# Attention pairs with more in flight, merge weights turned on the matmul engine, gates by Silu, and three smaller moves in a hybrid attention and HGRN2 block

## The chip, the cores and the metric

One core of a Trainium2 chip runs the whole program in one launch. The metric is the device time of one execution in microseconds (us). The kernel before has a median of 1483.52 us over three runs (1483.29 to 1485.46).

## The reference, cut to what matters

One encoder layer on x (1024 tokens, 1024 channels), all in float32:

```python
h = rms_norm(x, norm_w);  z = h @ w_in                     # 1024 -> 12288 columns
qkv_a, g_a, q_b, zf_fwd, zf_bwd, i_b, g_b, zgate_a, zgate_b = split(z)
for g, (window, dilation) in enumerate(((128, 1), (512, 4), (2048, 16))):
    q, k = rms_norm(q_g), rms_norm(k_g)                    # 8 heads of 64 per group
    s = q @ k + bias, banded;  m = max(s);  p = exp(s - m);  den = sum(p);  o_g = p @ v / den
M = max over g of m_g;  w_g = den_g * exp(m_g - M)
o_a = sum(w_g * o_g) / sum(w_g)                            # the three groups merged per head
y_a = (o_a * silu(g_a)) @ w_proj_a
f = lb + (1 - lb) * sigmoid(zf)                            # 8 heads of 128, forward and backward
o_b = rms_norm(gated_scan_fwd + gated_scan_bwd) * silu(g_b)
y_b = o_b @ w_proj_b
out = x + (sigmoid(zgate_a) * y_a + sigmoid(zgate_b) * y_b) @ w_out
```

## The kernel before

**Products.** A float32 product is made of three matmuls on rounded halves: each operand is split into a high part (ScalarE copies it into the rounded type) and a low part (the difference), and the kernel adds high x high, high x low and low x high. One matmul is 128x128 weights against 512 columns. The low part of a weight page (128x512, 256 KB) is made in one of three ways: a subtraction on GpSimd, a subtraction on VectorE, or, for `low = "dma"`, ScalarE writes minus the high part and a GpSimd-issued DMA adds the page to it from HBM.

**Stages.** In order: norm of x and the value columns of the three groups (to about 150 us); the block stage (to 631 us), where the input projection is done in blocks of four weight pages with seven block products instead of eight (named 11, T1, T2, 21, T3, 22, T4, twelve matmuls each; `run_quads`); a stage of ordinary groups `gp`, 24 matmuls into one PSUM bank each, for the columns i_b and the queries q_b, into which the attention is interleaved (to about 850 us) and then the merge of the three groups (to about 940 us); the HGRN2 stage, head after head between the `gp` groups of the forget gates (to about 1270 us); the two branch projections and the output projection, the last two again with seven block products (`seven`; names sA and sE).

**Block stage.** A block is normal `q`/`k` columns (`qk`, 12 of them, followed by the head norm on ScalarE and VectorE), branch gates (`sg`), HGRN2's g_b (`gb`) or the attention's g_a (`ga`). The results go to HBM; silu(g_a) and silu(g_b) are made later: `ga_sig` and `ga_mul` in the merge, `gate` in the HGRN2 stage, each a Sigmoid on ScalarE and a product on VectorE.

**Attention.** The work goes in 24 pairs of 128-query slabs with four heads. For a pair, TensorE computes scores (`sc`), VectorE adds the bias and takes the maximum in one operation (`as`), ScalarE takes eight exponentials (`exps`, with the row sum read out after each), TensorE turns the result (`transpose_p`, `pT`), ScalarE and VectorE copy it (`apt`), and TensorE multiplies it by the values (`pv`, `o`); ScalarE copies that out (`aos`). `left["in"]` counts pairs between scores and values, `left["out"]` those behind, and the conditions on them in `scores` and `transpose_p` set how many pairs overlap.

**Merge.** Maximum and sum of the groups 1 and 2 go to HBM and back in the order of tokens (`stats_out`, `stats_in`), `alphas` makes one weight per token, head and group, `alphas_out` turns three tiles on TensorE, and the result goes to HBM and back once more (`alD`, `alL`) to come to 16 partitions. A unit of the merge (eight: four head pairs by two halves of the tokens) spreads the weights with three 16-row matmuls (`al`) and multiplies, adds and gates on VectorE and GpSimd (`spread_al`).

**What sets the order.** All instructions are written out by a planner (`Builder`) that keeps a modelled time for each engine (`Plan.note` has the cost of each operation) and issues a task when its inputs are due and its `room` condition holds. Small TensorE pieces ("products" such as `sc`, `pT`, `o`, `al`, `U`) are put between the large matmuls, after every three to six of them, when the plan says that they are ready. The engines then run their lists in order; where reality is later than the plan, an engine waits.

Every instruction is recorded by one helper, so all have its line (57), and the profile's groups are told apart by tile names: `gp`, `qA`, `qE`, `qC`, `sA`, `sE` are PSUM tiles of large products, `whi`/`wlo` weight halves, `xh`/`xl` and `hh`/`hl` those of the data, `ob` and `acc` the data of the branch projection.

Of the kernel before, what the change touches and what calls it, by code (L numbers as in the profile page):

```python
# [18 lines left out]
S = 1024  # L19
# [9 lines left out]
EARLY = 8  # L29
QRAW, SPARE = 6, 7  # L30
LOWS = ("T2", "T4")
SQ, EA = 2, 6
VR, PT = 16, 7
# [81 lines left out]
class Plan:  # L115
# [25 lines left out]
    def note(self, key, op, args, kw):  # L141
# [30 lines left out]
        else:  # L172
# [12 lines left out]
            elif key == "act":  # L185
                pace = 0.09 + n / 1200.0
                need = {AF.Sigmoid: ("sig",), AF.Ln: ("ln",), AF.Exp: ("exp", "ln")}.get(args[2])
# [396 lines left out]
def hybrid_block(ctx, tc, a, out):  # L584
# [47 lines left out]
    for k in range(6):  # L632
        blocks += qk[2 * k:2 * k + 2] + sg[k:k + 1] + ([("gb", k)] if k < 4 else [])
    blocks += [("ga", 0), ("ga", 2)]

    def block_pages(kind, *at):
        if kind == "sg":
            return (*gate_pages(*at), *gate_pages(at[0], at[1] + 1))
        if kind == "ga":
            return tuple(some(72 + 2 * at[0], 4))  # L640
        if kind == "gb":
# [11 lines left out]
    for h in range(EARLY):  # L653
        items += q_pages(h)
# [151 lines left out]
    alD = dr.tile([3, 2, 8, 8, 128], F32, name="alD")  # L806
# [309 lines left out]
    def put_raw(dst):  # L1116
        def f(half, col, z, mine):
            ring = stage
            if not mine:
                ring, ps, z = blk["spare"], z, blk["spare"].get()  # L1120
                a_.activation(z, ps, AF.Copy)
# [4 lines left out]
            b.task("sp", [z], out, 1)  # L1126
# [3 lines left out]
    put_ga = lambda j: put_raw(lambda col, half: gaD[j + col, half])  # L1130
    put_gb = lambda k: put_raw(lambda col, half: gbD[2 * k + col, half])
# [6 lines left out]
    b.run_quads(A, [{"qk": put_qk, "sg": put_sg, "ga": put_ga, "gb": put_gb}[x[0]](*x[1:]) for x in blocks],  # L1138
# [7 lines left out]
    def attention_start(now=False):  # L1146
# [17 lines left out]
        for g in range(3):  # L1164
            for hv in range(2):
                soon = lambda n, k=2 * g + hv: att[n].soon() and (k == 0 or b.wire())
# [52 lines left out]
    def score_tasks(g, hv):  # L1219
# [61 lines left out]
    def exps(g, hv, i0, u, ss, neg, geo):  # L1281
        n, c0 = geo[u][1:3]
        for h in range(4):
            a_.activation(ss[u][:, h, c0:c0 + n], ss[u][:, h, c0:c0 + n], AF.Exp, bias=neg[:, u, h:h + 1],
                          accum_out=mst[g][:, 1, i0 + u, 4 * hv + h:4 * hv + h + 1])
        if u == 0:
            left[g, hv, i0] = []
        m = left["m", g, hv, i0]
        b.product(1, [ss[u]], lambda: transpose_p(g, hv, i0, u, ss[u], [x[3] for x in geo]),
                  lambda: left["out"] == m and att["pt"].soon(2 if g < 2 else 1), banks=2 if g < 2 else 1)  # L1290

    def transpose_p(g, hv, i0, u, s, slabs):
# [30 lines left out]
        if u == 0:  # L1323
# [6 lines left out]
                  and (b.bank.room(5 if g < 2 else 3) and b.bank.when(5 if g < 2 else 3) <= b.p.t["pe"] or not b.small))  # L1330
# [30 lines left out]
    vleft = {}  # L1361
# [9 lines left out]
    def merge_maybe(now=False):  # L1371
# [8 lines left out]
        mer["sel"] = sel = mer["p"].tile([16, 4, 128], F32R, name="sel")  # L1380
        half = lambda k: ident[0:16, 8 * k:8 * k + 8].rearrange("p (a j) -> p a j", a=4)[:, :, :, None].to_broadcast([16, 4, 2, 64])
        v_.tensor_tensor(sel.rearrange("p a (j c) -> p a j c", j=2), half(0), half(1), op=OP.add)
        mer["og"] = b.ring(mer["p"], "og", 6, [128, 512])
        mer["gal"] = b.ring(mer["p"], "gal", 2, [128, 512])
        mer["gas"] = b.ring(mer["p"], "gas", 2, [128, 512])
        merge_start()

    def stats_out():
        for g in (1, 2):
            for k in range(2):  # L1390
                if g == 1:
                    for half in range(2):
                        a_.dma_start(
                            _dram(stD, ((g * 2 + k) * S + 512 * half) * 8, [[32, 128], [8, 4], [1, 8]]),
                            mst[g][:, k].rearrange("p (r e) h -> p e r h", e=2)[:, half])
                else:
                    a_.dma_start(_dram(stD, (g * 2 + k) * S * 8, [[64, 128], [8, 8], [1, 8]]), mst[g][:, k])

    def stats_in():
        for g in (1, 2):  # L1400
            for k in range(2):
                a_.dma_start(nst[g][:, k], stD[g, k].rearrange("(t p) h -> p t h", p=128))
        nst["in"] = True

    nst = {0: mst[0]}

    def alphas():
        M = mer["p"].tile([128, 8, 8], F32, name="mM")
        v_.tensor_tensor(M, nst[0][:, 0], nst[1][:, 0], op=OP.max)
        v_.tensor_tensor(M, M, nst[2][:, 0], op=OP.max)  # L1410
        den = mer["p"].tile([128, 8, 8], F32, name="mden")
        tmp = mer["p"].tile([128, 8, 8], F32, name="mtmp")
        es = []
        for g in range(3):
            e = mer["p"].tile([128, 8, 8], F32, name=f"me{g}")
            v_.tensor_tensor(e, nst[g][:, 0], M, op=OP.subtract)
            a_.activation(e, e, AF.Exp)
            es.append(e)
            v_.tensor_tensor(tmp if g else den, e, nst[g][:, 1], op=OP.mult)
            if g:  # L1420
                v_.tensor_tensor(den, den, tmp, op=OP.add)
        v_.reciprocal(den, den)
        for g in range(3):
            v_.tensor_tensor(es[g], es[g], den, op=OP.mult)
            x = mer["p"].tile([128, 2, 8, 8], F32R, name=f"mx{g}")
            a_.activation(x[:, 0], es[g], AF.Copy)
            v_.tensor_tensor(x[:, 1], es[g], x[:, 0].bitcast(F32), op=OP.subtract)
            es[g] = x
# [964 lines left out]
```

## Time and profile before

| | |
|---|---|
| median of three runs | 1483.52 us |
| the profiled execution, its own time | 1483.24 us |
| its span in the profile | 1481.5 us |
| granted TensorE clock | 0.999 |
| TensorE (PE) busy | 1463.4 us, 99% of the span |
| VectorE (DVE), ScalarE (ACT), GpSimd (POOL) busy | 976.3, 897.6, 369.2 us |
| DMA | 227.76 MB, 154 GB/s on average |

Between the span and the execution's own time lie 1.7 us at the start and the end. The end of a matmul is modelled in these records, so that two matmuls overlap in them: what one costs is seen from start to next start, not from its listed length.

### The profile page before, as it was taken

How to read it: one execution, taken by the hardware profiler on the slowest of the kernel's cores; microseconds unless marked ns; L12 is line 12 of the kernel's file. 1: busy time of each engine (PE TensorE's matmuls, PEld its weight loads, DVE VectorE, ACT ScalarE, POOL GpSimd, SP SyncE). 2: the span in 40 equal slices, each digit the busy share in tenths (PEclk: the TensorE clock that was granted, in tenths of full speed). 3: DMA queues.
4: the chain of work that ended last, by engine and by line, in shares of the span. 5: the costliest groups of instructions: out<-in, count | busy, mean ns of one | idle time of the engine just before them, and what ended most of it. 6: DMA issues, size and time to landing. Idle time of an engine off the chain costs nothing. (4 is left out here: it accounts for less than half of the span.)

```text
span 1481.5 us, 23010 instructions
## 1 busy us (share of the span) xinstructions
PE 1463.4 (99%) x7965; PEld 1201.1 (81%) x7965; DVE 976.3 (66%) x1890; ACT 897.6 (61%) x1889; POOL 369.2 (25%) x374
## 2 busy tenths in 40 slices
PE   8999999999999999999999999999999999999998
PEld 7788888888888888877887787788888888787887
DVE  6792676768676788434443427488988886359973
ACT  5543665657474767346766632398887885556461
POOL 0031335455433334400200324322222221000011
PEclk9999999999999999999999999999999999999999
DMA  6465567686624342475644467743445443775565
GB/s 205 133 193 166 171 199 164 160 187 130 157 79 141 79 121 79 140 260 178 202 147 143 137 159 229 225 105 92 124 98 143 108 130 91 226 230 156 162 166 134
DMA packets 193579, 227.76 MB, mean 154 GB/s; under 512 B 45564, under 2 KB 118292, under 8 KB 192949
## 3 DMA queue, kind: packets, MB, share of 16 engines
q1 hardware_dynamic: 174084, 204.06, 43.6%
q0 software_dynamic: 11952, 21.76, 9.9%
q10 hardware_dynamic: 7424, 0.45, 0.3%
q8 instruction: 63, 1.03, 0.3%
q14 instruction: 56, 0.45, 0.1%
HBM read 166.08 MB, written 81.63 MB: 167 GB/s over the span
## 5 line engine op out<-in xcount | busy, mean ns | idle before, releaser
L57 POOL TENSOR_TENSOR wlo<-qraw,whi 128x512 fp32r<-128x512 f32 x120 | 174.8, 1466 | 299.9 <-ACT whi L57 255.9
L57 ACT ACTIVATE whi<-qraw 128x512 fp32r<-128x512 f32 x168 | 104.4, 627 | 92.3 <-DVE qraw L57 40.3
L57 PE MATMUL gp<-hh,whi 128*128 128x512 f32 x336 | 139.0, 414 | 0.7 <-ACT stage L57 0.7
L57 PE MATMUL gp<-hh,wlo 128*128 128x512 f32 x336 | 131.7, 392 | 0.0
L57 PE MATMUL gp<-hl,whi 128*128 128x512 f32 x336 | 131.3, 391 | 0.0
L57 POOL TENSOR_TENSOR wlo<-raw,whi 128x512 fp32r<-128x512 f32 x48 | 66.4, 1389 | 235.8 <-ACT whi L57 233.9
L57 DVE CUSTOM_DVE_ANT_0 as<-sc,abias 128x192 f32<-128x192 f32 (+2 forms) x192 | 56.1, 348 | 100.5 <-PE sc L57 80.2
L57 DVE TENSOR_TENSOR qraw<-qraw,qraw 128x512 f32<-128x512 f32 x96 | 86.4, 901 | 35.4 <-POOL wlo L57 27.0
L57 PE MATMUL gp<-whi,hh 128*128 128x512 f32 x248 | 101.6, 410 | 2.1 <-ACT hh L57 1.4
L57 PE MATMUL gp<-whi,hl 128*128 128x512 f32 x248 | 97.6, 394 | 1.3 <-DVE hl L57 1.3
L57 PE MATMUL gp<-wlo,hh 128*128 128x512 f32 x248 | 97.5, 393 | 0.0
L57 ACT ACTIVATE whi<-raw 128x512 fp32r<-128x512 f32 x104 | 64.9, 625 | 50.8 <-PE gp L57 33.5
L57 ACT ACTIVATE as<-as,neg 128x192 f32<-128x192 f32 (+2 forms) x192 | 83.5, 440 | 6.6 <-DVE neg L57 6.6
L57 ACT ACTIVATE stage<-gp 128x512 f32<-128x512 f32 x60 | 35.5, 594 | 82.0 <-PE gp L57 57.8
L57 DVE SCALAR_TENSOR_TENSOR ny<-ny,spare 128x512 f32<-128x512 f32 x48 | 76.0, 1584 | 1.6
L57 PEld LDWEIGHTS gp<-hh,whi 128*128 128x128 f32 x336 | 63.2, 188 | 14.9 <-ACT stage L57 1.8
L57 PE MATMUL qA<-hh,whi 128*128 128x512 f32 x192 | 75.1, 391 | 0.0
L57 PE MATMUL qA<-hh,wlo 128*128 128x512 f32 x192 | 75.0, 391 | 0.0
L57 PE MATMUL qA<-hl,whi 128*128 128x512 f32 x192 | 74.7, 389 | 0.0
L57 PEld LDWEIGHTS gp<-hh,wlo 128*128 128x128 f32 x336 | 63.0, 188 | 14.1
L57 PEld LDWEIGHTS gp<-hl,whi 128*128 128x128 f32 x336 | 63.4, 189 | 10.5
L57 ACT ACTIVATE ny<-ny 128x512 f32<-128x512 f32 x96 | 60.8, 633 | 6.5 <-DVE ny L57 3.4
(299 smaller groups left out, 4102.3 us busy)
## 6 DMA issues: line engine op xcount, KB each, us to landing
raw<-in_w_in_dram SPq DMA_DIRECT2D x96, 256.0 KB, 3.0
qraw<-in_w_in_dram SPq DMA_DIRECT2D x96, 256.0 KB, 4.2
qkD<-ny SPq DMA_DIRECT2D x48, 256.0 KB, 2.8
sg<-sgD SPq DMA_DIRECT2D x32, 256.0 KB, 2.7
eraw<-wsD SPq DMA_DIRECT2D x32, 256.0 KB, 3.0
wlo<-in_w_in_dram POOLq DMA_DIRECT2D x31, 256.0 KB, 4.2
sgD<-stage SPq DMA_DIRECT2D x26, 256.0 KB, 2.0
ak<-qkD SPq DMA_DIRECT2D x6, 1024.0 KB
```

The source lines that it names most:

```text
L57: got = f(*args, **kw)
```

## The change

Six things change. (1) **Queries in the block stage**: of the eight heads' q_b columns, those of heads 0 to 3 become two blocks (`qb`) of the block stage instead of eight `gp` groups. (2) **Silu in the block stage**: the `gb` and `ga` blocks move behind all `qk` blocks and are stored as silu(z), one Silu on ScalarE each; `ga_sig`, `ga_mul`, `gate` and `gates` go. (3) **Attention**: groups are taken in the order 1, 2, 0; three pairs instead of two may be in flight, a pair's transposes may come before the values product of the pair ahead, and that product no longer waits for free banks; 14 value tiles instead of 16, 8 `apt` tiles instead of 7; the plan's cost of an exponential with row sum rises by 0.07, that of a bias-and-maximum falls by 0.08. (4) **Merge**: `stats_out` runs for a group as soon as its last exponentials are planned, on SP's queue; the weights are put at 32-partition steps into one tile and turned by eight TensorE transposes, so that the trip to HBM and back goes; the spreading matmuls have 128 rows; 9 and 3 load buffers instead of 6 and 2, and two of its own for the result. (5) **Low parts by transfer**: eight weight pages of the branch projection (T1 and T3) get their low part by the DMA way instead of VectorE. (6) A line is added at the top, so the helper's line is 58.

```diff
+QB = 4
-VR, PT = 16, 7
+VR, PT = 14, 8
...
                 if kw.get("accum_out") is not None:
-                    pace += 0.12
+                    pace += 0.19
...
                 if op == "tensor_tensor_reduce":
-                    pace = 0.076 + _free(ins[0]) / 960.0 + 0.08
+                    pace = 0.076 + _free(ins[0]) / 960.0
...
-        blocks += qk[2 * k:2 * k + 2] + sg[k:k + 1] + ([("gb", k)] if k < 4 else [])
-    blocks += [("ga", 0), ("ga", 2)]
+        blocks += qk[2 * k:2 * k + 2] + sg[k:k + 1] + ([("qb", k)] if k % 2 == 0 and k < QB else [])
+    blocks += [("gb", k) for k in range(4)] + [("ga", 0), ("ga", 2)]
...
-    def put_raw(dst):
+    def put_raw(dst, silu=False):
...
-                a_.activation(z, ps, AF.Copy)
+                a_.activation(z, ps, AF.Silu if silu else AF.Copy)
...
+            if mine and silu:
+                b.task("act", [z], lambda: (a_.activation(z, z, AF.Silu), b.task("sp", [z], out, 1)), 2)
+            else:
+                b.task("sp", [z], out, 1)
...
-        for g in range(3):
+        for o, g in enumerate((1, 2, 0)):
...
-                      lambda: left["in"] < 2 and att["s"].soon(2), banks=4 if g < 2 else 2)
+                      lambda: left["in"] < 3 and att["s"].soon(2), banks=4 if g < 2 else 2)
...
+        done[g] = done.get(g, 0) + 1
+        if done[g] == 16 and g:
+            b.task("sp", [mst[g]], lambda: stats_out(g), 2)
...
-                  lambda: left["out"] == m and att["pt"].soon(2 if g < 2 else 1), banks=2 if g < 2 else 1)
+                  lambda: left["out"] >= m - 1 and att["pt"].soon(2 if g < 2 else 1), banks=2 if g < 2 else 1)
...
-                  and (b.bank.room(5 if g < 2 else 3) and b.bank.when(5 if g < 2 else 3) <= b.p.t["pe"] or not b.small))
+                  )
...
+    def alphas_out():
+        ab = mer["p"].tile([128, S], F32R, name="alB")
+        for half in range(2):
+            p = bank("alT")
+            for t in range(4):
+                t_.transpose(p[:, 128 * t:128 * t + 128], mer["x"][:, 4 * half + t].bitcast(F32), ident)
+            a_.activation(ab[:, 512 * half:512 * half + 512], p, AF.Copy)
         mer["ab"] = ab
...
-            t_.matmul(al[g], mer["sel"][:, p, :], mer["ab"][:, g, 512 * half:512 * half + 512], start=True, stop=True)
+            t_.matmul(al[g], mer["sel"][:, g, p, :], mer["ab"][:, 512 * half:512 * half + 512], start=True, stop=True)
...
     def logs(h):
...
-        if h:
-            gates(h - 1)
...
+    BY_DMA = ("T1", "T3")
...
-                b.split(raw[op, i])
+                b.low = "dma" if op in by_dma else "dve"
+                b.split(raw[op, i], page=pages[op][i])
...
-    seven_weights(b.ops, quad[0], SEVEN, {"11": obs})
+    seven_weights(b.ops, quad[0], SEVEN, {"11": obs}, BY_DMA)
```

Three places in the order of the instructions. The first is TensorE in the attention, before and then changed, where one pair's values product meets another's scores (`o` takes `apt` and the values `av`; `sc` takes keys `ak` and queries `aq`; `pT` turns `as`; "x2" is two alike):

```order
L57 MATMUL gp_6178<-whi_5547,hbl 128x512
L57 MATMUL o_6186<-apt_6142,av_5768 64x128 x2
...
L57 MATMUL o_6186<-apt_6158,av_5772 64x128 x2
L57 MATMUL sc_6208<-ak_5885,aq_5923 128x192
...
L57 MATMUL sc_6211<-ak_5885,aq_5923 128x256
L57 MATMUL gp_6178<-whi_5568,hbh 128x512
```

```order
L58 MATMUL pT_6452<-ident,as_6265 128x128 x4
L58 MATMUL sc_6470<-ak_6197,aq_6235 128x192
...
L58 MATMUL sc_6473<-ak_6197,aq_6235 128x192
L58 MATMUL gp_6246<-whi_5948,hh_104 128x512
L58 MATMUL gp_6246<-wlo_5949,hh_104 128x512
L58 MATMUL gp_6246<-whi_5948,hl_105 128x512
L58 MATMUL o_6505<-apt_6424,av_6066 64x128 x2
...
L58 MATMUL o_6505<-apt_6463,av_6068 64x128 x2
L58 MATMUL gp_6246<-whi_5969,hh_104 128x512
```

Before, `o` and the next `sc` stand side by side between large matmuls. Now `sc` follows transposes directly and `o` stands alone between large matmuls.

The second is the statistics of the merge, which stood on ScalarE's list and now stand on SP's (`stD` is HBM, `nst` the tile on the chip, `mst` the statistics; `stage` and `ibD` belong to `gp` groups):

```order
L57 ACTIVATE stage_8240<-gp_8171 128x512
L57 ACTIVATE whi_8243<-raw_8007 128x512
L57 DMA stD<-mst_107 512x1x8 x4
L57 DMA stD<-mst_108 128x64 x2
L57 DMA nst_8261<-stD 128x8x8 x2
L57 DMA nst_8262<-stD 128x8x8 x2
L57 ACTIVATE stage_8316<-gp_8269 128x512
```

```order
L58 DMA ibD<-stage_8333 128x512
L58 DMA oD<-aos_8353 128x2x256
L58 DMA ibD<-stage_8381 128x512
L58 DMA nst<-stD 128x8x8 x4
L58 DMA og_8416<-oD 128x512
L58 DMA og_8418<-oD 128x4x128
```

The stores of the statistics have gone far ahead; the four loads now stand behind the store `ibD<-stage_8381`, whose tile is that of the first whole `gp` group after the attention's last `o`.

The third is VectorE in the branch projection, where the block product T1 takes over from T2 (`ob<-ob,ob` makes T1's data and `xl` its low part; `wlo` is a low part of a weight page; before and then changed):

```order
L57 TENSOR_TENSOR ma_12860<-acc_13259,ma_12860 128x512
L57 TENSOR_TENSOR ma_12881<-acc_13297,ma_12881 128x512
L57 TENSOR_TENSOR ob_13048<-ob_13048,acc_13210 128x512
L57 TENSOR_TENSOR ob_13050<-ob_13050,acc_13233 128x512
L57 TENSOR_TENSOR wlo_13475<-eraw_13406,whi_13474 128x512
L57 TENSOR_TENSOR ob_13081<-ob_13081,acc_13257 128x512
L57 TENSOR_TENSOR ob_13083<-ob_13083,acc_13350 128x512
L57 TENSOR_TENSOR ob_13111<-ob_13111,ob_13191 128x512
L57 TENSOR_TENSOR wlo_13503<-eraw_13413,whi_13502 128x512
L57 TENSOR_TENSOR ob_13146<-ob_13146,ob_13203 128x512
L57 TENSOR_TENSOR xl_13517<-ob_13111,xh_13516 128x512
```

```order
L58 TENSOR_TENSOR ma_12799<-acc_13188,ma_12799 128x512
L58 TENSOR_TENSOR ob_12990<-ob_12990,acc_13173 128x512
L58 TENSOR_TENSOR acc_13223<-acc_13223,sg_13091 128x512
L58 TENSOR_TENSOR ob_12992<-ob_12992,acc_13205 128x512
L58 TENSOR_TENSOR ob_13024<-ob_13024,acc_13302 128x512
L58 TENSOR_TENSOR ob_13052<-ob_13052,ob_13138 128x512
L58 TENSOR_TENSOR ob_13101<-ob_13101,ob_13143 128x512
L58 TENSOR_TENSOR ob_13121<-ob_13121,ob_13151 128x512
L58 TENSOR_TENSOR xl_13402<-ob_13052,xh_13401 128x512
```

The `wlo` rows between have gone; between the first `acc<-sE` of product 21 and T1's first `xl` there were nine of them and one is left.

More of the change, by code (lines that the diff above doesn't have):

```diff
@@ L640, in block_pages @@
             return tuple(some(72 + 2 * at[0], 4))
+        if kind == "qb":
+            return (*q_pages(at[0]), *q_pages(at[0] + 1))
         if kind == "gb":
@@ L652, in hybrid_block @@
         items += ib_pages(k)
-    for h in range(EARLY):
+    for h in range(QB, EARLY):
         items += q_pages(h)
@@ L1401, in stats_in @@
             for k in range(2):
-                a_.dma_start(nst[g][:, k], stD[g, k].rearrange("(t p) h -> p t h", p=128))
-        nst["in"] = True
-    nst = {0: mst[0]}
+                s_.dma_start(mer["st"][:, g, k], stD[g, k].rearrange("(t p) h -> p t h", p=128))
     def alphas():
[L1408 to L1413, printed above, removed]
-        for g in range(3):
[L1415 to L1428, printed above, removed]
-        b.product(0, es, lambda: alphas_out(es), merge=False)
@@ L1445, in al_round @@
-    def al_round(ar):
-        ab = mer["p"].tile([16, 3, S], F32R, name="alB")
-        for g in range(3):
-            a_.activation(ab[:, g], ar[:, g], AF.Copy)
+        nst = mer["st"]
+        flat = lambda t: t.rearrange("p t h -> p (t h)")
+        M, den = (mer["p"].tile([128, 64], F32, name=n) for n in ("mM", "mden"))
+        e, w = (mer["p"].tile([128, 3, 64], F32, name=n) for n in ("me", "mw"))
+        part = lambda k: nst[:, :, k].rearrange("p g t h -> p g (t h)")
+        v_.tensor_tensor(M, flat(nst[:, 1, 0]), flat(nst[:, 2, 0]), op=OP.max)
@@ L1449, in al_round @@
+        b.product(0, [mer["x"]], alphas_out, merge=False, banks=2)
+    def alphas_out():
+        ab = mer["p"].tile([128, S], F32R, name="alB")
+        for half in range(2):
+            p = bank("alT")
+            for t in range(4):
+                t_.transpose(p[:, 128 * t:128 * t + 128], mer["x"][:, 4 * half + t].bitcast(F32), ident)
+            a_.activation(ab[:, 512 * half:512 * half + 512], p, AF.Copy)
         mer["ab"] = ab
@@ L1483, in merge_load @@
         b.product(4, [], lambda: spread_al(p, half, ld),
-                  lambda: len(ld) == 4 and "ab" in mer and b.p.done(mer["ab"]) + 4.0 <= b.p.t["pe"]
-                  and b.when_all(list(ld.values())) and stage.soon(),
+                  lambda: len(ld) == 4 and "ab" in mer and b.p.done(mer["ab"]) <= b.p.t["pe"]
+                  and b.when_all(list(ld.values())) and mer["acc"].soon(),
                   merge=False, banks=3)
@@ L1500, in spread_al @@
         v_.tensor_tensor(acc, acc, ld[3], op=OP.mult)
-        store(oaD[p, half], acc)
+        b.task("sp", [acc], lambda: (s_.dma_start(oaD[p, half], acc), mer["acc"].done(acc)), 1)
         mer["out"] = mer.get("out", 0) + 1
@@ L1507, in merge_start @@
     def merge_start():
-        for g in (1, 2):
-            nst[g] = mer["p"].tile([128, 2, 8, 8], F32, name=f"nst{g}")
-        stats_out()
-        b.task("act", [stD], stats_in, 3)
-        b.task("dve", [], alphas, 3, lambda: "in" in nst and b.when_all([nst[1], nst[2]]))
+        mer["st"] = st = mer["p"].tile([128, 3, 2, 8, 8], F32, name="nst")
+        stats_in()
+        a_.activation(st[:, 0], mst[0], AF.Copy)
+        b.task("dve", [st], alphas, 3)
         for k in range(8):
@@ L1550, in hybrid_block @@
         pos += 8
-    for h in range(EARLY):
+    for h in range(QB, EARLY):
         for u in range(2):
@@ L1920, in scale_out @@
         b.product(7, [on], lambda: out_transpose(h, u, on),
[L1921 removed]
+                  lambda: stage.soon() and (h, u) in GB and b.when_all([GB[h, u]]), merge=False)
     def out_transpose(h, u, on):
```

100 lines of the change are left out of this document (38 added, 62 removed).

## The prediction, made before the changed kernel ran

> **What bounds the kernel now.** I read the page first, then the table by stretches, then the waits of TensorE. In that table the columns after the stretch and its length are busy time and instructions of PE, PEld, DVE, ACT and POOL, then the granted clock, DMA share and GB/s; a row of waits gives the total, the number and the longest.
>
> ```profile
> PE 1463.4 (99%) x7965; PEld 1201.1 (81%) x7965; DVE 976.3 (66%) x1890; ACT 897.6 (61%) x1889; POOL 369.2 (25%) x374
> 111.00:148.00 37.00, 37.00 (x164) 30.57 (x163) 9.23 (x14) 11.19 (x18) 5.22 (x5) 1.00 0.53 167
> 629.00:851.00 222.00, 219.42 (x1792) 178.71 (x1791) 95.56 (x480) 143.34 (x493) 29.77 (x36) 1.00 0.54 178
> 1332.00:1369.00 37.00, 34.83 (x145) 26.58 (x144) 34.37 (x57) 24.97 (x45) 0.00 (x0) 1.00 0.51 162
> ...
> PE sE L57 <- DVE xl L57: 1.1, 3, 0.7
> PE sE L57 <- ACT xh L57: 1.0, 2, 0.5
> ...
> PE oB L57 <- DVE S L57: 0.8, 1, 0.8
> ...
> PE U L57 <- ACT kT L57: 0.4, 2, 0.2
> ...
> PE oB L57 <- DVE xa L57: 0.4, 1, 0.4
> ```
>
> TensorE bounds every stage: an undisturbed stretch holds 164 large matmuls in 37.00 us, 0.2256 us each, and the waits shown are at most 0.8 each. In 1332 to 1369 VectorE is 93% busy and TensorE gets 145 in: the one place with another engine at the bound. So the time follows from three things: how many matmuls TensorE issues, what they lose at changes of shape, and which waits come or go. Work taken from ScalarE, VectorE or DMA counts only through these.
>
> **Queries in the block stage.** Eight `gp` groups of 24 matmuls go (192). Two blocks of seven products with twelve matmuls come (168). 24 x 0.2256 = **-5.4**, as certain as anything here: the matmuls run end to end in both stages. What the two blocks ask of ScalarE is a copy per result and of VectorE the sums of a block, in a stage that already runs 24 such blocks.
>
> **Shape changes in the attention.** Starts of neighbours on TensorE:
>
> ```profile
> 706.39 0.39 PE L57 MATMUL gp<-whi,hbl 128*128 128x512 f32 x1
> 706.71 1.97 PE L57 MATMUL o<-apt,av 128*64 128x128 f32 x32
> 708.61 1.78 PE L57 MATMUL sc<-ak,aq 64*128 64x256 f32 x16
> 710.32 0.50 PE L57 MATMUL gp<-whi,hh 128*128 128x512 f32 x1
> 710.66 0.39 PE L57 MATMUL gp<-wlo,hh 128*128 128x512 f32 x1
> ...
> 711.59 0.40 PE L57 MATMUL gp<-whi,hl 128*128 128x512 f32 x1
> 711.83 1.91 PE L57 MATMUL pT<-ident,as 128*128 128x128 f32 x16
> 713.49 0.47 PE L57 MATMUL gp<-whi,hh 128*128 128x512 f32 x1
> ...
> 1245.22 0.60 PE L57 MATMUL onT<-ident,on 128*128 128x128 f32 x4
> 1245.75 1.09 PE L57 MATMUL X<-qr,km 128*64 128x128 f32 x16
> ...
> 1155.05 0.60 PE L57 MATMUL onT<-ident,on 128*128 128x128 f32 x4
> 1155.40 0.47 PE L57 MATMUL gp<-hh,whi 128*128 128x512 f32 x1
> 1155.72 0.39 PE L57 MATMUL gp<-hl,whi 128*128 128x512 f32 x1
> ```
>
> A `gp` matmul before `o` lasts 0.32 (706.39 to 706.71), +0.09; the first after `sc` 0.34, +0.11; before `pT` 0.24, nothing. No row has `sc` right behind `pT`; the nearest is `X` behind `onT`, also transposes followed by a half shape: 0.53 against 0.35 with `gp` behind, where the `gp` pays 0.32 instead. Net 0.18 - 0.09 = +0.09. In the two orders the neighbour `o` to `gp` goes from 2 to 24 places, `o` to `sc` from 22 to 0, `pT` to `sc` or `o` from 0 to 23, `gp` to `o` or `sc` from 25 to 24. 22 x 0.11 + 23 x 0.09 - 0.09 = **+4.4**. Bounds: 2.4 if a change behind `pT` is free, as that from `gp` to `pT` is; 7.8 if each of 45 costs 0.17, the whole excess of 0.53 over 0.35.
>
> The Trainium skill, "TensorEngine Tiling (Array Packing)", section "Tiling Modes", speaks against this part of the change: switching the mode drains TensorE. It prices nothing; the rows above agree for entry and return (0.09, 0.11).
>
> **Waits in the attention.** A pair is a chain. ScalarE copies `pT` and takes eight exponentials:
>
> ```profile
> 706.06 0.49 ACT L57 ACTIVATE as<-as,neg 128x256 f32<-128x256 f32 x1
> ...
> 709.50 0.49 ACT L57 ACTIVATE as<-as,neg 128x256 f32<-128x256 f32 x1
> ...
> 709.99 0.57 ACT L57 ACTIVATE aos<-o 128x512 f32<-128x512 f32 x1
> ...
> 702.91 1.32 ACT L57 ACTIVATE apt<-pT 128x512 f32<-128x512 f32 x2
> ```
>
> Eight take 3.9 us (706.06 to 709.99). With `apt` 1.3, `aos` 0.5 and a weight page or an eviction 0.5, a 256-wide pair needs ScalarE for 6.2 us; TensorE needs 1.90 + 1.71 + 1.66 for `o`, `sc`, `pT` and about 2.2 for nine `gp`, 7.5. With a third pair in flight the exponentials of one overlap the values of another, so I expect TensorE to stay in the lead, but covers shrink from six `gp` to three. I take **+1.0**, bounds -2 (the old waits near this stage go) and +12 (the first rival).
>
> **Merge weights.** In the kernel before:
>
> ```profile
> 855.20 4.03 ACTq L57 DMA_DIRECT2D nst<-stD  x4
> ...
> 862.28 1.35 DVE L57 TENSOR_TENSOR mM<-mM,nst 128x64 f32<-128x64 f32 x1 [2.47 <-DMA nst<-stD]
> ...
> 868.87 0.23 DVE L57 TENSOR_TENSOR mx<-me,mx 128x64 fp32r<-128x64 f32 x1 [0.32 <-ACT mx L57]
> ```
>
> The statistics took 7.1 us from first load to last landing (855.20 to 862.28) and the arithmetic 6.8 (to 869.1). The stores now go early. The loads wait on SP behind a store whose tile is the first whole `gp` group after the last `o`: 24 x 0.2256 + 0.6 of eviction = 6.0, up to 6.9 with the store's issue. With 7.1 for the loads and 4 to 5 for the shorter arithmetic (three chains became one wide one) the transposes are ready 17.1 to 19.0 after the last `o`. Ahead of them stand 72 `gp`, 16.4 with their entry. So TensorE waits 0.7 to 2.6 at `alT`, where before 114 `gp` and more covered it: **+2.0**. Bounds: 0 if the loads land a little sooner, 4.4 if the arithmetic still takes 6.8 (6.9 + 7.1 + 6.8 - 16.4).
>
> Eight transposes replace three, 5 x 0.104 (1.66 / 16 above): **+0.5**. The spreading matmul:
>
> ```profile
> 884.14 0.39 PE L57 MATMUL gp<-hh,wlo 128*128 128x512 f32 x1
> 884.46 0.96 PE L57 MATMUL al<-alB,sel 16*128 16x512 f32 x3
> 885.35 0.50 PE L57 MATMUL gp<-hh,whi 128*128 128x512 f32 x1
> 885.69 0.40 PE L57 MATMUL gp<-hl,whi 128*128 128x512 f32 x1
> ```
>
> Entry 0.32, three in 0.89, return 0.34: against plain matmuls that is 0.89 + 0.09 + 0.11 = 1.09 against 0.69. With 128 rows there is no change of shape: 8 x 0.40 = **-3.2**.
>
> A second page would take that gain away: by "TensorE: Matmul & The Clock Gate", section "Why this matters for your kernels", of the Trainium skill, a single matmul with few rows takes as long as one with 128. For the matmul alone the rows put that at 0.89 against 0.69; entry and return (0.20) it does not cover. By the page the sum would be some 1.6 us higher.
>
> **Low parts by transfer.** At the hand-over to T1:
>
> ```profile
> 1351.62 0.40 PE L57 MATMUL sE<-xh,whi 128*128 128x512 f32 x1
> 1352.68 0.50 PE L57 MATMUL sE<-xl,whi 128*128 128x512 f32 x1 [0.67 <-DVE xl L57]
> ...
> 1358.02 0.39 PE L57 MATMUL sE<-xh,whi 128*128 128x512 f32 x1
> ...
> 1332.02 2.49 DVE L57 TENSOR_TENSOR wlo<-eraw,whi 128x512 fp32r<-128x512 f32 x4
> ```
>
> Twelve steps took 6.40 us where twelve plain ones (0.233 here) take 2.80: 3.6 lost, each at `xh` or `xl`, which follow VectorE's list. Four `wlo` take 2.49, 0.60 each from start to start; eight fewer of them ahead of the first `xl` bring it 4.8 us forward. The eight pages now pass GpSimd's queue, idle here (0.00 in the stretch), and ScalarE, 67% busy. I take **-3.0**, bounds -3.6 and 0: the transferred page may be late instead.
>
> **Gates by Silu.**
>
> ```profile
> L57 ACT ACTIVATE gs<-gb 128x512 f32<-128x512 f32 x16 | 9.7, 622 | 0.1
> L57 DVE TENSOR_TENSOR gb<-gb,gs 128x512 f32<-128x512 f32 x16 | 10.8, 688 | 7.7 <-ACT gs L57 7.7
> L57 ACT ACT_TABLE_LOAD x33 | 42.3, 1283 | 3.7 <-DMA gb<-gbD 1.9 <-PEq L2377 1.2
> ```
>
> 20.5 us leave two engines which TensorE covers, and ten table loads go. What that is worth is TensorE's waits in the HGRN2 stage, 1.6 in the three rows shown at the top (`oB`, `U`, `oB`): **-1.0**, bounds -1.6 and +2, if data read later than now makes a new one (four of the size of that 0.4 to 0.8). Seven fewer changes to half shapes between `gp`, `X` and `Y` there: **-0.7**. In the block stage 18 Silus and eight neighbourhoods of two tables (1.28 each) hang on ScalarE behind results: **+0.5**, bounds -0.5 and +3, hidden as long as the banks of a block cover 1.3 us.
>
> **The sum.** -5.4 + 4.4 - 3.2 + 0.5 - 0.7 - 3.0 - 1.0 + 2.0 + 1.0 + 0.5 = -4.9. The profiled execution took 1483.24, 0.3 under the median of 1483.52: **1478.3 us**, 0.35% less.
>
> **Rivals.** *Slower: the attention becomes bound by the chain over ScalarE.* Between a pair's last `pT` and the next use of its `apt` stand 1.3 of copies and, in front of them on ScalarE, part of another pair's 3.9 of exponentials: 3.5 to 3.7, against covers of three `gp` and one product, 3.3 to 3.7. Of 24 pairs each may lose 0.25 (5.9) before the gain is gone and 0.37 (8.9) before it can be told as slower; at 0.5 the stage loses 12 and the time is 1489. For it: the wider exponential pairs and only three `gp`. Against: 219.42 busy of 222.00 before, with two in flight. 0.10.
>
> *About the same: changes and late weights eat the gain.* Each new neighbour at 0.17 adds 3.4, or `alT` waits its 4.4 and the transferred lows come as late as the `xl` did (+3.0): 1480.5 to 1484. For it: no row shows `pT` before `sc`. 0.20.
>
> *Better: the waits vanish as well.* -1.6 and -3.6 in full, `alT` at 0, the attention at -2, changes at 2.4: 1470 to 1474. For it: all bounds of small terms lie that way when ScalarE is freed. 0.15.
>
> The forecast itself, 1474 to 1480.5, has 0.55. A measurement of this kernel tells about 0.2% (3 us) from no change. Faster is forecast and the better case, 0.70; the same 0.20; slower 0.10. The range takes half of the better case and most of the same one: 1472 to 1483.5.
>
> **What would show it.** A wait of 0.7 to 2.6 us of `alT` on DVE or ACT near 830 to 870. No wait of `sE` on `xl` or `xh` near 1350. A first `gp` behind `o` at 0.34, and `sc` behind `pT` some 0.2 later than a `gp` would be. `al` spaced 0.23 with plain neighbours. 23 table loads. 24 fewer large matmuls. I am wrong if `pT`, `o` or `sc` show waits of over 9 us in all, if the block stage gets longer by more than the two added blocks (168 matmuls, 37.9 us), or if `sE` now waits for `wlo`.

## The result, and the profile after

The changed kernel takes 1475.02 us, median of six runs (1473.25 to 1475.58), against 1483.84 us for the kernel before (1483.27 to 1486.98): a ratio of 0.9935, 95% interval 0.9922 to 0.9948. It is faster, by 8.8 us; 5.2 were forecast. The profiled execution has a span of 1472.7 us where the kernel before had 1481.5.

TensorE is still the bound. Here are four stretches cut at the same places of the program (start of the block stage, its end, the last `al`, the end of the HGRN2 stage, the last matmul): first of the kernel before, then of the changed one. The columns are those of the prediction's table.

```profile
149.19:631.11 481.92, 481.51 (x2114) 396.27 (x2112) 343.78 (x403) 295.66 (x506) 201.30 (x155) 1.00 0.52 140
631.11:935.26 304.15, 301.57 (x2140) 242.56 (x2138) 138.63 (x535) 168.81 (x537) 55.20 (x54) 1.00 0.59 184
935.26:1272.85 337.59, 334.25 (x2226) 283.82 (x2225) 254.61 (x545) 261.31 (x538) 78.60 (x125) 1.00 0.48 122
1272.85:1476.71 203.86, 201.66 (x864) 161.86 (x864) 141.23 (x226) 100.76 (x176) 10.35 (x12) 1.00 0.63 182
```

```profile
148.76:673.18 524.42, 520.78 (x2281) 427.63 (x2280) 354.25 (x421) 319.56 (x547) 217.25 (x165) 1.00 0.50 136
673.18:934.30 261.12, 257.99 (x1946) 207.84 (x1945) 133.00 (x525) 153.13 (x510) 44.90 (x47) 1.00 0.64 200
934.30:1268.50 334.20, 332.14 (x2233) 285.85 (x2231) 246.14 (x531) 241.74 (x514) 79.21 (x126) 1.00 0.49 125
1268.50:1468.47 199.97, 199.97 (x863) 162.52 (x864) 133.46 (x215) 101.54 (x180) 17.26 (x20) 1.00 0.67 191
```

These lengths mix what was moved with what was gained. So I take from each stretch 0.2265 us for every large matmul that starts in it (most neighbours in these traces start 0.226 or 0.227 apart) and call the rest its residue: the small products, the changes of shape and the waits. The head norm's sums `nss`, one matmul of the same size each, count as large. Cut finer, from the first start of one kind to the first start of the next:

| stretch | residue before | after | difference | forecast |
|---|---|---|---|---|
| 24 large matmuls fewer (x 0.2265) | | | -5.4 | -5.4 |
| block stage | 3.5 | 8.0 | +4.5 | +0.5 |
| attention, with the `gp` before it | 119.9 | 124.5 | +4.6 | +5.4 |
| last `o` to last `al` | 10.6 | 7.8 | -2.9 | -0.7 |
| last `al` to the end of the HGRN2 stage | 119.8 | 115.2 | -4.7 | -1.7 |
| last two projections, first `sE` to last matmul | 6.4 | 2.8 | -3.6 | -3.0 |
| all else (start, first `gp` of the projections, end) | | | -1.2 | 0 |
| sum | | | -8.7 | -4.9 |

The forecast's sum was short by 3.8. Behind that lie errors of 4 and 3 us of opposite sign, and one of 2.

TensorE's waits of the changed kernel, the largest rows that are new (`nss` is the head norm's sum, in the block stage):

```profile
PE nss L58 <- ACT whi L58: 1.6, 1, 1.6
...
PE nss L58 <- DVE nlo L58: 1.2, 2, 0.9
...
PE nss L58 <- DVE ny L58: 0.8, 1, 0.8
```

The rows of `sE` on `xl` and `xh`, of `U` and of `kT` have gone. Four waits at `nss` have come, 3.6 us by these rows and 4.3 counted from start to start (4.7 with the slower step behind each), which is about the whole rise of the block stage's residue. The other new rows are small: 0.7 at the attention's first `sc` and 0.3 at `Y`. In the attention and the merge of the changed kernel:

```profile
803.46 0.50 PE L58 MATMUL gp<-whi,hh 128*128 128x512 f32 x1
803.80 0.40 PE L58 MATMUL gp<-wlo,hh 128*128 128x512 f32 x1
...
804.26 1.03 PE L58 MATMUL pT<-ident,as 128*128 128x128 f32 x8
805.23 2.00 PE L58 MATMUL sc<-ak,aq 64*128 64x256 f32 x16
...
885.80 1.04 PE L58 MATMUL alT<-ident,mx 128*128 128x128 f32 x8
886.59 0.48 PE L58 MATMUL gp<-hh,whi 128*128 128x512 f32 x1
...
888.05 0.85 PE L58 MATMUL al<-alB,sel 128*128 128x512 f32 x3
888.74 0.39 PE L58 MATMUL gp<-hh,whi 128*128 128x512 f32 x1
```

The first `gp` behind an `o` takes 0.34 (803.46 to 803.80), and eight transposes followed by `sc` take 0.97 where eight followed by `gp` take 0.79: the prices of the forecast (0.11, and 0.18 less the 0.09 that the `gp` no longer pays). `alT` starts right behind its `gp`, with no wait. The three `al` take 0.69 to the next start, 0.23 each.

### The profile page after: what moved, and what is told of

Same layout as the page of the kernel before. It is cut to its first block, busy times and chain, and to the rows that moved or that the text cites. A ratio compares the mean times of both kernels' runs of the same rounds, so it can differ in the third digit from the quotient of the medians.

```text
span 1472.7 us, 22977 instructions
## 1 busy us (share of the span) xinstructions
PE 1454.8 (99%) x7946; PEld 1200.0 (81%) x7946; DVE 964.9 (66%) x1872; ACT 886.8 (60%) x1884; POOL 382.4 (26%) x385
## 3 DMA queue, kind: packets, MB, share of 16 engines
q0 software_dynamic: 13104, 23.86, 10.6%
## 5 line engine op out<-in xcount | busy, mean ns | idle before, releaser
L58 POOL TENSOR_TENSOR wlo<-qraw,whi 128x512 fp32r<-128x512 f32 x130 | 190.0, 1467 | 326.2 <-ACT whi L58 288.3
L58 ACT ACTIVATE whi<-qraw 128x512 fp32r<-128x512 f32 x182 | 113.0, 626 | 88.8 <-DVE qraw L58 44.8
L58 DVE TENSOR_TENSOR qraw<-qraw,qraw 128x512 f32<-128x512 f32 x104 | 93.2, 896 | 41.2 <-POOL wlo L58 31.4
L58 PE MATMUL gp<-hh,whi 128*128 128x512 f32 x288 | 118.4, 411 | 0.0
L58 PE MATMUL gp<-hh,wlo 128*128 128x512 f32 x288 | 113.1, 393 | 0.0
L58 PE MATMUL gp<-hl,whi 128*128 128x512 f32 x288 | 112.5, 391 | 0.0
L58 POOL TENSOR_TENSOR wlo<-raw,whi 128x512 fp32r<-128x512 f32 x40 | 56.0, 1412 | 98.3 <-ACT whi L58 98.2
L58 DVE TENSOR_TENSOR wlo<-qraw,whi 128x512 fp32r<-128x512 f32 x52 | 35.9, 690 | 55.3 <-ACT whi L58 55.3
L58 DVE COPY apt<-pT 128x512 f32<-128x512 f32 (+2 forms) x42 | 27.7, 664 | 65.1 <-PE pT L58 65.1
L58 PEld LDWEIGHTS gp<-hh,wlo 128*128 128x128 f32 x288 | 54.1, 188 | 11.8
```

The costliest lines, as they stand in the source:

```text
L58: got = f(*args, **kw)
```

## The experiments

The differences below are those of medians, against 1475.0 for the changed kernel, and of residues in the profiled execution. Two cautions. The kernel before, timed again beside each group of runs, took 1483.84, 1484.40, 1485.09 and 1484.99 us, so a difference of about 1 us between medians of different groups means little; the ratios to the kernel before do not have this error. And the block stage of the changed kernel, with its instructions untouched, had residues of 8.0, 7.3, 7.8 and 10.7 in the changed kernel and three runs below, so that differences there of under 3 us mean little by themselves.

Not everything was undone alone. The merge's turned weights with their earlier statistics, the order of the attention's groups, the buffer counts and the two costs in the plan were not; what is said of them rests on rows of before and after.

**The overlap of the attention undone.**

```diff
-lambda: left["in"] < 3 and att["s"].soon(2)
+lambda: left["in"] < 2 and att["s"].soon(2)
-lambda: left["out"] >= m - 1 and att["pt"].soon(...)
+lambda: left["out"] == m and att["pt"].soon(...)
 # and the condition on free banks ahead of pv put back
```

> The changed kernel with the attention's three limits put back (two pairs in flight, a pair's transposes only behind the values of the pair ahead, the values only with free banks); the group order 1, 2, 0 and all else stay. The instruction order then has `o` followed by `sc` 22 times again, no `pT` followed by `sc` or `o`, 342 large matmuls between the pieces instead of 240, and 66 instead of 72 between the last `o` and `alT`. Theory: the overlap itself only costs, 0.19 us a pair of shape changes, 4.3 us in all, and its waits were no worse before; without it the time is 1475.0 - 4.3 = 1470.7 (1469 to 1472.5). Rival: with fewer large matmuls left for the merge and the first HGRN2 head the limits bring back waits of 3 us or more there or in the attention: 1474 to 1478, with waits of `alT`, `al`, `pT` or `U` in the profile that the changed kernel has not.

Measured: 1488.36 us, 13 more, ratio to the kernel before 1.0024 (1.0012 to 1.0037). The attention's own residue fell as the theory said, from 122.5 to 118.9. The merge lost far more:

```profile
PE al L58 <- DVE og L58: 10.2, 5, 4.4
...
927.19 1.31 PE L58 MATMUL al<-alB,sel 128*128 128x512 f32 x5
932.85 0.50 PE L58 MATMUL al<-alB,sel 128*128 128x512 f32 x1 [4.36 <-DVE og L58]
...
938.31 0.79 PE L58 MATMUL al<-alB,sel 128*128 128x512 f32 x1 [2.61 <-DVE og L58]
...
905.30:943.80 38.50, 27.67 (x109) 20.39 (x107) 28.92 (x32) 4.70 (x8) 13.55 (x10) 0.87 0.85 265
```

With two pairs in flight the attention uses 342 large matmuls as cover instead of 240. Since the queries have gone to the block stage, only 84 are then left between the `al` (180 in the changed kernel), the merge runs into VectorE, and TensorE stands waiting. From the first to the last `al` the residue is 19.5 instead of 5.5: 10.2 us of waits and some 4 of slow steps behind them. (The profiled execution was the shortest of the eight, 1485.83 us; what the others lost beyond it no trace shows.) My theory that the overlap only costs was wrong, and the rival named the right place but a much smaller loss: the overlap spends 4 us on shapes and gives the merge back about a hundred matmuls of cover.

**Without the query blocks, and both undone.** Two runs, QB = 0 alone, and QB = 0 with the old limits.

```diff
-QB = 4
+QB = 0
```

> The changed kernel without the two query blocks: the queries of heads 0 to 3 are eight `gp` groups again, between the attention and the HGRN2 stage, and every pair of qk blocks has only one sg block behind it. 24 large matmuls more: +5.4. Theory (head norms too dense in the block stage): the waits at `nss` grow beyond the 4.3 us of the changed kernel, to 6 or more, since the fillers are fewer still; 1475.0 + 5.4 + 2 = 1482 (1480 to 1485). Rival (the query blocks themselves bring the waits, by their pages or the stage tiles): `nss` waits fall under 1 us, 1475.0 + 5.4 - 4 = 1476.5. Either way `alT` and `al` have more cover and wait no more than in the changed kernel.

> The same without the query blocks and with the attention's three old limits (two pairs in flight). The overlap theory, after the 14 us that TensorE waited at `al` when only the limits were put back: the overlap costs 4 us in the attention and is worth its price only where the queries have gone from the cover of the merge. With them back, 180 or more large matmuls stand among the `al` again, `al` waits under 2 us, and this runs 3 to 5 us faster than the one without query blocks and with three pairs in flight. Rival (the waits at `al` come from two pairs in flight as such, not from the cover): `al` waits about 10 us here too, and this runs 6 us or more slower than that one.

Measured: 1493.29 us, above the range of the theory, and 1490.19 us. In the second `al` waits 1.2 us in all (10.2 above), with 150 large matmuls among the `al` (180 were expected), and it is the faster of the two by 3.1 by the medians. That this lies in the expected 3 to 5 is in part luck. The two profiled executions are 6.8 apart: 1.4 of that lies between the block stage and the HGRN2 stage (residues of 131.5 and 130.0), where the overlap acts, and 4.5 in the block stage and 1.0 in the last projections, where both have the same instructions. So the waits at `al` come from the missing cover and not from two pairs as such, and without the query blocks the overlap pays nothing; by the residues it costs 1.4. Queries and overlap belong together; neither is worth its measured share alone.

The block stage of the first run shows what else the query blocks do. It waits

```profile
PE nss L58 <- ACT whi L58: 6.3, 2, 3.9
PE nss L58 <- ACT nhi L58: 5.5, 1, 5.5
```

and its residue is 24.1 instead of 8.0 (19.6 in the second run). This kernel's g_b blocks stand at the end, so without query blocks every pair of `qk` blocks has one other block behind it. Fewer fillers, more waits: the density theory, more strongly than I expected it.

**The gates back, and then the order of the blocks.** First only g_b's gate goes back to the HGRN2 stage; then, in addition, its four raw blocks go back between the `qk` blocks, and the query blocks behind all `qk` blocks.

```diff
-put_gb = lambda k: put_raw(lambda col, half: gbD[2 * k + col, half], True)
+put_gb = lambda k: put_raw(lambda col, half: gbD[2 * k + col, half])
 # and gate(h, u), gates(h) as in the kernel before
 # second run, in addition:
-    blocks += qk[...] + sg[k:k + 1] + ([("qb", k)] if k % 2 == 0 and k < QB else [])
-blocks += [("gb", k) for k in range(4)] + [("ga", 0), ("ga", 2)]
+    blocks += qk[...] + sg[k:k + 1] + ([("gb", k)] if k < 4 else [])
+blocks += [("qb", k) for k in range(0, QB, 2)] + [("ga", 0), ("ga", 2)]
```

> The changed kernel with g_b stored as it is and its gate made in the HGRN2 stage again, by Sigmoid and a product (g_a stays by Silu, the blocks stay where they are). The instruction order of TensorE in the HGRN2 stage is then that of the kernel before: 99 stretches of large matmuls instead of 89, `gp` to `X` 8 instead of 4 times. Theory: the HGRN2 stage's gain of 5.0 us comes from the gates alone, some 2 to 2.5 from the ten stretches less and 1.5 to 2 from waits: 1475.0 + 4.5 = 1479.5 (1478 to 1481). Rival: it comes from the other changes (queries of heads 0 to 3 long in HBM, the loads of the merge): 1474.5 to 1476.

> The changed kernel with g_b stored as it is (no Silu, gate in the HGRN2 stage) and its four blocks back behind the first four sg blocks; the query blocks stand behind all qk blocks. Against the run with g_b stored as it is but left behind the qk blocks (1478.8) only the order of blocks differs. Density theory: the `nss` waits (3.0 us there by groups) go under 1 and the time is 1478.8 - 3.5 = 1475.3 (1474 to 1476.5). Rival: the waits have another cause and stay, 1478 to 1480.

Measured: 1478.80 us (0.9969, 0.9958 to 0.9980) and 1475.33 us (0.9935, 0.9922 to 0.9947), both inside what the theory gave. In the first the residue from the last `al` to the end of the HGRN2 stage is 119.2, against 115.2 in the changed kernel and 119.8 before: 4.1 of the 4.7 us come from g_b's gates. The second run has 119.2 there too. TensorE's waits there are those of the kernel before again:

```profile
PE oB L58 <- DVE S L58: 0.8, 1, 0.8
...
PE U L58 <- ACT kT L58: 0.4, 2, 0.2
PE oB L58 <- DVE xa L58: 0.4, 1, 0.4
```

In the second the only wait left in the block stage is this one, and its residue is 3.9 (6.6 in the first run, 3.5 in the kernel before); no execution of it took as long as the shortest of the first run:

```profile
PE qA L58 <- ACT stage L58: 0.7, 2, 0.5
```

So the gates by Silu bring 4.1 us in the HGRN2 stage, and the order of blocks that they need costs as much in the block stage (8.0 against 3.9): g_b's part of that move is worth nothing (1475.33 with neither, 1475.02 with both).

**Silu between the `qk` blocks.** Why must the Silu blocks stand at the end? Two runs with all of g_b by Silu: its blocks back between the `qk` blocks, and all blocks alternating.

```diff
 # first run
+    blocks += qk[2 * k:2 * k + 2] + sg[k:k + 1] + ([("gb", k)] if k < 4 else [])
+blocks += [("qb", k) for k in range(0, QB, 2)] + [("ga", 0), ("ga", 2)]
 # second run
+rest = [sg[0], ("qb", 0), sg[1], ("qb", 2)] + sg[2:] + [("gb", k) for k in range(4)] + [("ga", 0), ("ga", 2)]
+for k in range(12): blocks += [qk[k], rest[k]]
+blocks += rest[12:]
```

> The changed kernel with the four g_b blocks back between the qk blocks (behind the first four sg blocks) and the two query blocks at the end; g_b still by Silu. Theory: TensorE's four new waits at `nss` (4.3 us in all) come from qk blocks that follow each other with only one other block between the pairs, so that a head norm is not through when the next needs ScalarE and VectorE; with two other blocks between, as in the kernel before, they fall under 1 us and the time is about 1471.5 (1470 to 1473), although Silu in the middle of the norm costs some table loads of 1.28 us on ScalarE. Rival: the waits come from the Silus or the added blocks, or the table loads put in new ones: `nss` waits of 3 us or more, 1474.5 to 1478.

> The changed kernel with the blocks alternating: one qk block, one other block, twelve times, the two g_a blocks last. Theory (density of the head norm): every qk block has a whole block without norm behind it, waits at `nss` under 1 us, 1471.5 (1470 to 1473). Rival: a norm spreads over more than one block whatever stands between, or the Silu's table loads matter: 1474 to 1478.

Measured: 1583.40 and 1500.47 us. My theory fell: I had put the table loads at a few. Group of table loads, and waits of TensorE, of the first run:

```profile
L58 ACT ACT_TABLE_LOAD x107 | 137.3, 1283 | 12.6 <-issue 9.6 <-PEq L2346 1.2
...
PE nss L58 <- DVE ny L58: 28.0, 5, 6.4
PE nss L58 <- ACT whi L58: 18.6, 4, 4.6
PE qA L58 <- ACT stage L58: 16.4, 5, 5.0
PE qA L58 <- ACT spare L58: 14.6, 6, 3.8
```

107 loads instead of 23, each 1.28 us on the engine that also makes every weight's high part: 84 more take 108 us, and the block stage's residue rises by 109, from 8.0 to 116.8. The second run has 60, and its residue is 32.1. Grouping the Silus is what makes them affordable, and the price of the grouping is the missing filler between the `qk` blocks.

**The query blocks elsewhere, and a late transfer.** Three runs: query blocks behind the second and third pair of `qk` blocks; the last two bias-table transfers later; both.

```diff
-([("qb", k)] if k % 2 == 0 and k < QB else [])
+([("qb", 2 * (k - 1))] if 1 <= k <= 2 else [])
 # second and, with the above, third run
-after=b.p.t["pe"] + 3.0 + 100.0 * g + 10.0 * k)
+after=b.p.t["pe"] + 3.0 + (0.0, 100.0, 335.0)[g] + 10.0 * k)
```

> The changed kernel with the two query blocks behind the second and the third pair of qk blocks instead of the first and the third. The first `nss` waits (313 and 354 us) fall where GpSimd issues its transfers of HBM to HBM (224 to 390 us) and VectorE's operations lengthen; two other blocks between the pairs there should take them away, about 2.8 of 4.3 us: 1472.2 (1471 to 1474). Rival: the waits only move to another pair: 1474.5 to 1477.

> The changed kernel with the last two of the six transfers that spread the bias tables (`skewD`, 768 KB each in 512 rows, at 272 and 286 us) issued about 235 us of the plan later, where the other DMA is low. Behind the second one the weight page `qraw` comes late (VectorE waits 1.5 us for it in the changed kernel, 10.4 in the run with the query blocks moved). Theory: lateness of weights joins density at 300: the waits at `nss` at 313 and 354 (2.8 together) go under 1, 1472.5 (1471.5 to 1474). Rival: density alone; the waits stay or new ones come behind the moved transfers, 1474.5 to 1477.

> Both: the query blocks behind the second and third pair of qk blocks, and the two bias-table transfers later. Theory: the 3.1 us that TensorE waited for `spare` at 305 followed from pages that came 10 us late behind the bias-table transfer; without it the block stage waits under 1 us in all, 1475.0 - 3.5 = 1471.5 (1470.5 to 1473). Rival: the waits only move on to where the transfers go, 1474 to 1477.

Measured: 1474.98, 1474.15 and 1472.22 us (1471.74 to 1474.39; ratio 0.9919, 0.9904 to 0.9934). The first two missed what the theories gave (1471 to 1474 and, by 0.15, 1471.5 to 1474), the third is inside (1470.5 to 1473). In the first the `nss` waits went but for 0.4, and one wait of 3.1 us came. Its rows on SP, VectorE and TensorE:

```profile
286.63 0.64 SPq L58 DMA_DIRECT2D skewD<-tabD  x1
287.36 10.96 SPq L58 DMA_DIRECT2D qraw<-in_w_in_dram  x4
...
301.99 0.69 DVE L58 TENSOR_TENSOR qraw<-qraw,qraw 128x512 f32<-128x512 f32 x1 [10.38 <-DMA qraw<-in_w_in_dram]
...
304.89 0.50 PE L58 MATMUL qA<-S2h,whi 128*128 128x512 f32 x1 [3.13 <-ACT spare L58]
```

Behind the bias-table transfer the four weight pages take 11 us to issue and VectorE stands 10.4 us for one of them. With that transfer moved, the third run has no wait of its block stage over 0.9 us, and a residue there of 4.7; the second alone keeps waits at `nss` (2.3 in all) and a residue of 6.0. So the rows name both causes, density and late pages, and taking both away gives the lowest median here. By the residues this is not settled for each cause alone: 7.5 and 6.0 lie within the scatter given above, and the run with g_b's blocks between the `qk` blocks had 3.9 with the transfers where they were. The third run's lead on the changed kernel is 2.8 us by the medians, 0.16% by the ratios, whose intervals overlap: by the spans and the waits it is better, by the times alone it is not settled. The first run also corrects a number of the expectations: `nss` waits alone do not tell what a stage loses, the bank may be waited for instead.

**Low parts by VectorE again.**

```diff
-BY_DMA = ("T1", "T3")
+BY_DMA = ()
```

> The changed kernel with the low parts of T1 and T3 of the branch projection made by VectorE again. Theory: the hand-over from T2 to T1 loses 3.6 us again, in waits of `sE` on `xl` and `xh` like those of the kernel before at 1352 to 1358, and the last part (first `sE` to the last matmul) takes 147.5 instead of 143.9: 1475.0 + 3.5 = 1478.5 (1477.5 to 1479.5). Rival: the rest of the change frees VectorE enough there: 1474.5 to 1476.

Measured: 1484.57 us, 9.6 more and equal to the kernel before (0.9996, 0.9985 to 1.0006). That is far above the 3.5 expected, and the place is another: not `sE` on `xl`, but once, one block product earlier, at the data of T2.

```profile
1346.46 0.80 PE L58 MATMUL sA<-xh,whi 128*128 128x512 f32 x1 [5.74 <-ACT xh L58]
...
1351.62 0.63 PE L58 MATMUL sA<-xh,wlo 128*128 128x512 f32 x1
1352.05 0.59 PE L58 MATMUL sA<-xh,whi 128*128 128x512 f32 x1
...
1346.00:1352.00 6.00, 5.54 (x12) 4.09 (x13) 4.54 (x8) 2.05 (x4) 0.00 (x0) 0.50 0.22 81
...
1343.72 0.70 DVE L58 SCALAR_TENSOR_TENSOR acc<-ob,ob 128x512 f32<-128x512 f32 x1
...
1345.26 0.63 ACT L58 ACTIVATE sg<-sg 128x512 f32<-128x512 f32 x1 [1.64 <-DMA sg<-sgD]
1345.80 0.62 ACT L58 ACTIVATE xh<-acc 128x512 fp32r<-128x512 f32 x1
```

In the changed kernel the same two operations stand here:

```profile
1332.49 0.69 DVE L58 SCALAR_TENSOR_TENSOR acc<-ob,ob 128x512 f32<-128x512 f32 x1
...
1333.64 0.62 ACT L58 ACTIVATE xh<-acc 128x512 fp32r<-128x512 f32 x1
```

`acc<-ob,ob` is T2's fourth tile of data, made by VectorE, and `xh<-acc` its high part. Counted from the first `sA` (1315.88 in this run, 1313.37 in the changed kernel), VectorE makes that tile 8.7 us later: from 1326.9 on it works with 0.3 us of idle time in all, and 13 of its 30 operations up to the tile are low parts of weights. The tile was ready at 1344.4. Then `xh` stood 1.4 us behind a gate on ScalarE whose page had come late. TensorE waited 5.7 us, and after it the granted clock was 0.50 for 6 us: a matmul took 0.43 (1351.62 to 1352.05) instead of 0.23. Wait and slow clock make 8.9 of the 9.1 us by which this last part's residue is longer (11.9 to 2.8). So what was forecast, low parts that stand ahead of data on VectorE's list, is what the run shows; the product that it hits and the price are others. The hand-over to T1 itself then shows no wait: it comes when TensorE is already late. So this run does not show the forecast's own 3.0 a second time.

**The spreading matmuls on 16 rows.**

```diff
-t_.matmul(al[g], mer["sel"][:, g, p, :], mer["ab"][:, 512 * half:512 * half + 512], ...)
+t_.matmul(al[g], mer["sel"][32 * g:32 * g + 16, g, p, :], mer["ab"][32 * g:32 * g + 16, 512 * half:512 * half + 512], ...)
```

> The changed kernel with the 24 spreading matmuls `al` on the 16 rows that hold a group's weights (rows 0, 32 and 64 on) instead of all 128. Theory: the 16 rows cost 0.4 us a unit by the change of shape at entry and return, as in the kernel before, and nothing inside: three take 0.89 to the next start and the `gp` behind 0.34: 1475.0 + 3.2 = 1478.2 (1477 to 1479). Rival: on three different groups of rows the three run side by side, as the Trainium skill says in its page TensorE: Matmul & The Clock Gate, section Why this matters for your kernels; then three take 0.55 or less and the time is 1475 to 1476.

Measured: 1478.68 us, inside the theory's range, and yet the theory is wrong. Its rows:

```profile
891.44 0.51 PE L58 MATMUL al<-alB,sel 16*128 16x512 f32 x3
891.87 0.50 PE L58 MATMUL gp<-hh,whi 128*128 128x512 f32 x1
892.21 0.39 PE L58 MATMUL gp<-hl,whi 128*128 128x512 f32 x1
...
PE nss L58 <- ACT whi L58: 3.5, 1, 3.5
...
PE sc L58 <- DMA av<-vD: 1.9, 1, 1.9
```

Three `al` take 0.43 to the next start: they run side by side, as the Trainium skill says of small products on different groups of 32 rows ("TensorE: Matmul & The Clock Gate", section "Why this matters for your kernels"). Entry and return cost 0.20 more (0.09 and 0.11), so that a unit takes 0.64 against 0.69 with 128 rows; from the first `al` to the matmul behind the last are 45.9 us against 46.5. The 3.7 us more lie elsewhere: in the block stage (residue 10.7, with one wait of 3.5 and a slowed clock behind it) and at the attention's first `sc`, in instructions that this edit does not touch. A time that falls in the expected range is no proof of the reason; the stage's own rows are. In the kernel before, all three stood on the same 16 rows, took 0.89, and so had no such gain.

## Why the prediction was right, and where not

The sign, the time (1475.0 in 1472 to 1483.5) and the bound were right: TensorE stayed the bound, and the sum of what it issues and waits for gave the change. By its steps:

- **Queries, -5.4: right** by count (5184 large matmuls before, 5160 after, `nss` left out), with two effects that the step left out: the blocks serve as fillers between head norms (24.1 of residue without them), and they take the cover from the merge (10 us of `al` waits when the overlap is undone).
- **Shape changes, +4.4, and waits in the attention, +1.0: right, a little high.** The residue rose by 4.6 with the `gp` before it, of which waits are some 0.5 and 3.7 lie in the attention itself; undoing the overlap took 3.7 off again. (The upper bound, 45 times 0.17, is 7.65 and not 7.8.) The slower rival (a chain over ScalarE) did not appear: no `pT` or `o` is in the list of waits.
- **Merge weights: `al` -3.2 and transposes +0.5 right** (0.69 for three, `gp` at 0.23 behind, and a residue among the `al` that is 3.3 smaller; 0.79 for eight transposes). **The wait of +2.0 at `alT` was mis-sized**: it is 0. The term that failed is "7.1 for the loads". That was the time of loads right behind their own stores on ScalarE's queue; on SP's, with the last store issued 70 us before, it is 3.9 (whether the queue or the stores make the difference no run tells):

```profile
875.31 2.36 SPq L58 DMA_DIRECT2D nst<-stD  x4
...
879.19 0.72 DVE L58 TENSOR_TENSOR mM<-nst 128x64 f32<-128x64 f32 x1 [5.54 <-DMA nst<-stD]
...
883.31 0.52 DVE L58 TENSOR_TENSOR mx<-me,mx 128x64 fp32r<-128x64 f32 x3 [0.39 <-ACT mx L58]
```

  The arithmetic took 4.6 (to 883.8), as forecast, and the transposes were due at 885.8. The zero was among the bounds ("if the loads land a little sooner").
- **Low parts by transfer, -3.0: right** in place and near in size (-3.6; the waits at the hand-over are gone). What its removal costs in the changed kernel is more and falls on T2, see above.
- **Gates: -1.0 for waits right, -0.7 for changes of shape mis-sized**, together -4.7, of which 4.1 by g_b's gates. TensorE's waits between the last `al` and the end of the HGRN2 stage fell from 2.4 to 1.3. The failing term is the count of seven changes: between the same two places the traces have 91 stretches of large matmuls before and 81 after, and 91 again with g_b's gates put back. Ten stretches at 0.20 for entry and return are at most 2.0 of the other 3.6; where the rest lies was not taken apart.
- **Block stage, +0.5 with a bound of +3: wrong**, +4.5. The prediction had named the sign for it: the stage got longer by 42.5 us, more than the 37.9 of the two added blocks. The step said that only Silu's table loads matter, "hidden as long as the banks of a block cover 1.3 us". The Silus stand where no norm runs and cost nothing visible. What it overlooked is what their move leaves behind: with g_b's blocks gone from between the `qk` blocks, the head norms of neighbours meet on ScalarE and VectorE. The instruction order showed the move; I had read from it only what comes in, not what filler goes out.

The errors of the block stage (+4.0), the gates (-3.0) and `alT` (-2.0) come from unrelated causes and cancel to -1.0. That they do is luck. The rest of the 3.8 is smaller misses of one sign: the attention, the low parts and the stretches that no step named. With 2.7 us more in the block stage, as the run with 16 rows had them there with the same instructions, the sum would have come within 1.1 of the forecast for no reason that is in it.

## What to carry to other kernels

Where one engine bounds everything, its large independent work is a stock of cover: an edit that removes some of it, or spends less of it in one stage, shows up as waits or as relief in the next stage, so edits that share this stock must be priced together. When work is moved for the sake of a table or a queue, ask what it was standing between. And a run whose time comes out as expected still needs its own stage's rows, since here one landed in the range by waits in code that it did not touch.

## What the runs showed of the hardware

- **In these runs a wait of TensorE could cost half again as much after it ended.** Of the waits of 3.4 us or more, each one (3.5, 3.7, 3.95, 4.7, 5.4, 5.7 among them) was followed by 6 to 14 slow steps, most of them 0.43 us instead of 0.23, some 1.2 to 2.8 us in all; a wait of 3.1 was not, those of 2.0 to 2.7 sometimes were, and those up to 1.9 never. The row of 1346 to 1352 above shows the granted clock at 0.50. The Trainium skill's rule in "TensorE: Matmul & The Clock Gate", section "Why this matters for your kernels", is to leave no gap of over some 3 us, and the runs agree for the long ones; the shorter ones that were followed by slow steps fall below it.
- **Shapes:** a change from a large matmul to a half shape cost 0.09, the first large matmul back 0.11; a change from a large matmul to transposes and back nothing. Transposes with a half shape behind took 0.17 to 0.18 more than with a large matmul behind, which then takes 0.09 more itself: 0.09 net.
- **VectorE beside GpSimd:** an operation of 0.69 us at best took 4.12 (5.38 in the kernel before) while GpSimd made low parts and issued transfers:

```profile
303.89 1.09 POOL L58 DMA_DIRECT2D wsD<-in_w_out_dram  x1
304.46 1.84 POOL L58 TENSOR_TENSOR wlo<-qraw,whi 128x512 fp32r<-128x512 f32 x1
...
302.73 4.12 DVE L58 SCALAR_TENSOR_TENSOR ny<-ny,spare 128x512 f32<-128x512 f32 x1
```

  In the changed kernel a head norm stands behind it, and the first `nss` wait follows; no run here tells how much of that wait is due to it. It does not make such a wait by itself: in the run with g_b's raw blocks between the `qk` blocks the operation took 5.37, and no `nss` waited.
